# One transformer-like layer on Trainium2: the order of loads, place products and the first gate product between the output projection and the experts

## The chip, the cores and the metric

The kernel runs on one core of one Trainium2 chip, as one launch. The metric is the device time of one execution in microseconds (us), the median of several runs. Engines are named as in the profile: PE is TensorE, DVE is VectorE, ACT is ScalarE, POOL is GpSimd, SP is SyncE, which here only issues DMAs. A change of 1% of this kernel is about 10.5 us.

## What is computed

One layer of a hybrid encoder over 512 tokens (16 learned meta tokens are put ahead of the stream; 512 rows in the kernel, four blocks of 128) of width 1024, in float32. After two mixer branches (a chunked state-space scan and a causal pooling), gated and summed, the end of the layer is what matters here:

```python
    mixed = (gates[:, :, 0] * y_ssd + gates[:, :, 1] * y_pool) @ w_out[i]
    h = layer_norm(DN_ALPHA * h + mixed, ln1_g[i], ln1_b[i])
    ffn = moe_ffn(h, w_router, w_exp_gate[i], w_exp_up[i], w_exp_down[i])
    h = layer_norm(DN_ALPHA * h + ffn, ln2_g[i], ln2_b[i])
...
def moe_ffn(x, w_router, w_gate, w_up, w_down):
    scores = jax.nn.softmax((t @ w_router).astype(jnp.float32), axis=-1)
...
    topv, topi = lax.top_k(jnp.where(in_grp, scores, -1.0), TOP_K)
...
    for e in range(N_EXPERTS):
        h = jax.nn.silu(t @ w_gate[e]) * (t @ w_up[e])
        out = out + comb[:, e:e + 1] * (h @ w_down[e])
```

Each token is sent to 2 of 16 experts (hidden width 512), both within one of four groups of experts.

## The kernel before

**Stages.** The span of 1045 us has four parts: the input projection and the scan (to about 655 us), the output projection `wo` with residual, layer norm and router (656 to 733 us), the sixteen experts one after the other (735 to 1010 us), and the last layer norm.

**Output projection and router.** The product with `w_out` is cut into four blocks of tokens (`t`) and two halves of 512 columns (`hf`): `out_mm(t, hf)` is 24 matmuls of 128x512 into one PSUM bank, numbered 0 to 23, three for each of 8 blocks of the contraction (both operands are split into a high and a low part). All of `hf=0` comes first, then `hf=1`. `post(t, hf)` on DVE adds the bank to the residual `vt[t]` (in the trace `v`), which is loaded from `h_dram`, and gathers layer norm statistics. When both halves of a block are there, `router(t)` runs as a generator in stages: (0, 1) PE transposes `v`, ACT copies it to `hT`; (2) PE makes the logits (`ss<-wrg,hT`), DVE finishes the layer norm's scale, ACT takes the exponential (`e`), DVE picks the two experts (`oha`, `ohs`); then PE counts each token's place in its expert (`ss<-ohs,tri`, the rank product); (3) DVE makes from the ranks a one-hot matrix for the first expert's rows (`R0`, in the trace `xg`) and `R`; PE scatters tokens and weights into slots by `ss<-to,R` (the place product, a matrix `iw` of expert by slot). PE keeps program order here, and the table `AT[t]` says behind which matmul of `out_mm(t, 1)` which router takes its next stage: `(12,1)` is "ahead of matmul 12, a stage of router 1". So the blocks of matmuls are the cover under which the routers' DVE and ACT work runs.

**Start of the experts.** `place(t)` builds the first expert's tokens transposed by matmul (`pso<-xg,v`), and `x_out` writes them to `xT`, its first four blocks on ACT and the last four on DVE. The other experts' tokens are gathered by an indirect DMA on POOL from `h1_dram`, transposed on PE (`pt<-ident,xg`) and written by `x_out` as well. From `iw` DVE makes the lists of tokens `idx`, and PE's two small products `ss<-iws,xg` with two select masks spread the slots over partitions (`ixq`, `wq`); four products `ss<-ohs,onesb` count tokens for each expert. After that DVE multiplies the normed `vt` by `g1B`, adds `b1B`, POOL stores them in `o_dram`, where the experts' outputs are added later, and DVE works out a list of overflow (`ov`). For an expert `i`, PE makes a gate product (`gu`, into PSUM: 16 matmuls of 32x256 for each of the two halves of the weights; the trace records a float32 matmul twice), an up product, a third block of slots, transposes and the down product; ACT and DVE do the silu and the multiplication.

**Buffers and queues.** The masks live in `xg1` (its columns 512 to 767), a tile under the tag `hL2`, whose earlier user is `wo`; so their first write waits until PE has read that weight for the last time. POOL's queue holds, in program order, the masks' `iota`, then the loads of `v`, of the first up weights (`raw`), of `g1B` and `b1B`. Nearly all weights come over SP's queue, one 1 MB DMA a half, into a ring of buffers `places`; a DMA waits in SP's queue until the ring's next buffer is free, and everything behind it waits too. The scheduler sets the order on engines other than PE where no explicit order stands.

Of the kernel before, what the change touches and what calls it, by code (L numbers as in the profile page):

```python
# [10 lines left out]
F32 = mybir.dt.float32  # L11
# [4 lines left out]
AF = mybir.ActivationFunctionType  # L16
# [4 lines left out]
D = 1024  # L21
# [27 lines left out]
RX = 5  # L49
# [8 lines left out]
GX = 1  # L58
AT = ((), ((6,0),(8,0),(14,0)), ((6,1),(8,1),(12,0),(14,1),(20,0)), ((6,2),(8,2),(12,1),(14,2),(20,1)))
LASTS = (3,3,"0",3,"1",2,"2",2,3,"3",3)  # L60
# [32 lines left out]
def hybrid_kernel(ctx, tc, x, meta_tokens, ln_in_g, ln_in_b, w_router, w_in, conv_w, conv_b,  # L93
# [175 lines left out]
    with ExitStack() as p1:  # L269
# [613 lines left out]
        def mix(t):  # L883

            MARK(f"mix{t}")
            c = slice(t * 128, (t + 1) * 128)
            mt = ga.tile([128, 2, KT, 128], F32R, name="mt", tag=("ze", "XP", "yHL", "M")[t])
            mixT.append(mt)
            for i in range(2):
                k4 = slice(4 * i, 4 * i + 4)  # L890
                ps = mm()[:, 0, :].rearrange("p (k c) -> p k c", k=4) if (t, i) in MXP else ss((128, 4, 128))
                for k in range(4):
                    T.transpose(ps[:, k, :], acc[t][:, (4 * i + k) * 128:(4 * i + k + 1) * 128], ident)
                m = grp.tile([128, 4, 128], F32, name="mix", tag="y")
                for q in range(2):
                    V.tensor_mul(m[:, 2 * q:2 * q + 2], ps[:, 2 * q:2 * q + 2], sg0[2 * i + q][:, :, c])
                (G if (t, i) in MA else V).tensor_add(m, m, pooled[i][:, :, c])
                A.copy(mt[:, 0, k4], m)
                (G if (t, i) in MS else V).tensor_sub(mt[:, 1, k4], m, mt[:, 0, k4])
# [38 lines left out]
        xg1 = hpool.tile([128, D], F32, name="xg1", tag="hL2")  # L938
        for i, pat in enumerate(([[32, 2], [0, 2], [1, 32]], [[0, 4], [1, 32]])):
            sel = xg1[:, 512 + 128 * i:640 + 128 * i]  # L940
            G.iota(sel, pattern=pat, base=64 * i, channel_multiplier=0, **exact)
            V.tensor_scalar(sel, sel, tokf[:, 0:1], None, op0=OP.is_equal)
        hb = hpool.tile([128, 2, 2048], F32, name="hb", tag="hH")
        early = [hpool.tile([128, 4, 512], F32, name="rawh", tag="hL0"), hb[:, 0, :].rearrange("p (k c) -> p k c", k=4)]
        with tc.high_priority():
            G_ = InOrder(tc, G)
            for t in range(NT):
                (Q if t < QV else G_).dma_start(vt[t], h_dram[t * 128:(t + 1) * 128, :])
                if t == FX:
                    rows2(G_, first, wu[order[0]], 512)  # L950
                if t == GX:
                    G_.dma_start(g1B, bcast_row(ln1_g, D))
                    G_.dma_start(b1B, bcast_row(ln1_b, D))

# [123 lines left out]
        def place(t):  # L1078
# [5 lines left out]
            for k in range(KT):  # L1084
                T.matmul(xps[k // 4][:, k % 4, :CAP], lhsT=cols2(vt[t], k), rhs=R0s[t][:, :CAP],
                         start=(t == 0 and k % 4 == 0), stop=(t == NT - 1 and k % 4 == 3))

        exs, R0s, r0_ins, xps = [], [], [], []
        post(0, 0, pso0)
# [7 lines left out]
        for r in LASTS:  # L1097
            if isinstance(r, str):
                place(int(r))
            else:  # L1100
                next(stages[r])
        T = T_
        with tc.high_priority():
            x_out(xps, CAP)

        def to_idx(dst, src):
# [9 lines left out]
        for i in range(2):  # L1116
# [4 lines left out]
            V.tensor_copy(wq[i], pq[:, 2 * NE * i + NE:2 * NE * (i + 1)])  # L1121
        G.memset(xg1, 0.0)
        g1 = gather(xg1, h1_dram[:, :], idx[:CAP, order[1]:order[1] + 1]).ins
# [5 lines left out]
        V.tensor_copy(cnt, pn[:, :NE])  # L1129
        c1 = V.tensor_copy(ctab, cnt[0:1]).ins  # L1130

        with tc.issue_after(c1), tc.issue_after(g1):
# [16 lines left out]
    def tile_of(pool, tag, **kw):  # L1149
# [6 lines left out]
              + [hb_(1)] + [tile_of(ga, t) for t in ("ze", "XP", "yHL", "M")]  # L1156
              + [tile_of(wsp, t, **two) for t in ("wh", "wl")] * 2 + [tile_of(rawz, "raw")] * RZ
              + [tile_of(hpool, "hL0"), tile_of(wsp, "wh3", **one), hb_(0), tile_of(rawx[RX - 1], "raw")])

# [32 lines left out]

    def quad(p, lhs, rhs, m, **kw):

        for j in range(4):
            last_['PE'] = T.matmul(p[BK * j:BK * (j + 1), m], lhsT=lhs(j), rhs=rhs(j), **kw).ins


    gu3 = psG.tile([128, 256], F32, name="gu3", bufs=1)
    py3 = psY.tile([128, 256], F32, name="py3")  # L1200

    def gu(ws):

        MARK("gu")
        ps = psG.tile([128, 256], F32, name="gu")
        for n in range(KT):
            w, k = ws[n // 4], n % 4
            quad(ps, lambda j: xT[:, n, BK * (j // 2):BK * (j // 2) + BK],
                 lambda j: w[:, k, 256 * (j % 2):256 * (j % 2) + 256], slice(0, 256),
                 start=(n == 0), stop=(n == KT - 1))  # L1210
        return ps

# [314 lines left out]
    for i, e in enumerate(order[:last]):  # L1527
        if i:
            gather(XG[(i + 1) % 2], h1_dram[:, :], ix_of(i + 1))
        wg2, wu2 = (fetch(wg[e], 512), fetch(wu[e], 512)) if i else (wg_, wu_)  # L1530
        pg = gu(wg2)
        if i:
            count(i)
            htr(hs.pop(i - 1))
        pu = gu(wu2)
        hs[i] = act(pg, pu, p3=gu_third(i, (wg2, wu2)))
        xprep(XG[(i + 1) % 2])
        if i:
            add_rows(down(i - 1, fetch(wd[order[i - 1]], 256)), i - 1)
# [107 lines left out]
```

## Time and profile before

| quantity | value |
|---|---|
| runs | 1046.36, 1048.78, 1055.65 us; median 1048.78 |
| profiled execution | 1047.15 us |
| its span, first to last instruction | 1045.4 us |
| PE busy | 948.9 us, 91% of the span |
| DVE, ACT, POOL busy | 586.2, 350.5, 165.5 us |
| mean granted clock of TensorE | 0.966 |
| HBM read and written | 185.01 and 19.01 MB |

The span is 1.75 us shorter than the execution. In the profile a clock of 1.00 is 2.4 GHz, 0.50 is 1.2 GHz. A timeline row has the start, the duration of the whole row, engine, line of the kernel, operation, out and in, and in brackets the idle time of the engine before it with what released it; a row with x16 stands for sixteen instructions on end, the duration being that of all. A window row has its busy time for each engine with the count of instructions.

### The profile page before, as it was taken

Reading aid. Unit: us, or ns where it says so; the run is one execution under the profiler, and the core shown is the slowest. Engines: PE = TensorE matmul, PEld = TensorE weight load, DVE = VectorE, ACT = ScalarE, POOL = GpSimd, SP = SyncE. Lnnn points to the kernel's source line nnn. Section 1 sums busy time; section 2 is a strip of 40 time slices with the busy share of each in tenths; the row PEclk is TensorE's granted clock in tenths of the full one; section 3 lists DMA queues with packets and bytes.
Section 4 is the critical chain, followed back from the end, with each engine's and each line's share of the span. In section 5 each row is a group of like instructions: output and inputs, shape, how many; then the busy total and the mean of one; then the engine's idle time right before and its main releaser. Section 6 shows DMA issues by size and latency. Waiting matters only on the chain. (4 is left out here: it accounts for less than half of the span.)

```text
span 1045.4 us, 19947 instructions
## 1 busy us (share of the span) xinstructions
PE 948.9 (91%) x8460; PEld 762.1 (73%) x8460; DVE 586.2 (56%) x1159; ACT 350.5 (34%) x507; POOL 165.5 (16%) x147
## 2 busy tenths in 40 slices
PE   4879999999999999999999898979989788999970
PEld 3878888999899898989898776868655345664540
DVE  6877661476869697878788788456611101010143
ACT  4344333432534262524334353123212121212252
POOL 4830000000000000000000245100213121212223
PEclk9989999999999999999999998989999999999995
DMA  7442436422323241423332333787699999999854
GB/s 216 139 161 99 133 128 176 121 85 95 119 86 130 71 147 58 139 84 122 102 122 101 128 125 126 309 319 292 187 390 366 374 372 367 373 377 361 290 145 81
DMA packets 98291, 198.92 MB, mean 190 GB/s; under 512 B 9948, under 2 KB 56644, under 8 KB 97168
## 3 DMA queue, kind: packets, MB, share of 16 engines
q1 hardware_dynamic: 83248, 163.25, 44.5%
q0 software_dynamic: 9088, 18.63, 7.0%
q10 hardware_dynamic: 5856, 15.61, 4.0%
q8 instruction: 76, 1.25, 0.5%
q14 instruction: 23, 0.19, 0.1%
HBM read 185.01 MB, written 19.01 MB: 195 GB/s over the span
## 5 line engine op out<-in xcount | busy, mean ns | idle before, releaser
L255 DVE TENSOR_TENSOR wl<-raw,wh 128x2048 fp32r<-128x2048 f32 (+1 forms) x49 | 111.7, 2283 | 53.5 <-ACT wh L252 53.4
L89 PE MATMUL gu<-raw,xT 128*32 128x256 f32 (+1 forms) x2752 | 132.7, 343 | 6.2 <-issue 4.2
L252 ACT CAST wh<-raw 128x2048 fp32r<-128x2048 f32 (+1 forms) x49 | 87.9, 1798 | 144.9 <-PE ss L800 64.1
L307 PE MATMUL mm<-hH,wh 128*128 128x264 f32 x624 | 129.0, 288 | 6.0 <-ACT ze L599 5.3
L307 PE MATMUL mm<-hH,wl 128*128 128x264 f32 x624 | 128.3, 287 | 0.0
L307 PE MATMUL mm<-hL,wh 128*128 128x264 f32 x624 | 127.7, 286 | 0.0
L89 PEld LDWEIGHTS gu<-raw,xT 128*32 128x32 f32 x2752 | 87.7, 110 | 47.0 <-issue 13.8
L1254 DVE TENSOR_TENSOR sg<-sg,gu 128x128 f32<-128x128 f32 x15 | 4.3, 287 | 205.0 <-ACT sg L1253 205.0
L307 PEld LDWEIGHTS mm<-hH,wh 128*128 128x128 f32 x624 | 99.4, 190 | 9.3 <-ACT ze L599 5.5
L809 POOL TENSOR_TENSOR acc<-acc,pre 128x512 f32<-128x512 f32 x12 | 19.2, 1617 | 531.2 <-ACT pre L808 531.2
L325 PE MATMUL mm<-hH,wh 128*128 128x512 f32 x256 | 102.7, 401 | 0.0
L325 PE MATMUL mm<-hL,wh 128*128 128x512 f32 x256 | 101.7, 397 | 0.0
L325 PE MATMUL mm<-hH,wl 128*128 128x512 f32 x256 | 101.6, 397 | 0.0
L307 PEld LDWEIGHTS mm<-hH,wl 128*128 128x128 f32 x624 | 98.3, 190 | 1.2
L307 PEld LDWEIGHTS mm<-hL,wh 128*128 128x128 f32 x624 | 97.6, 190 | 0.2
L89 PE MATMUL py<-raw,hT 128*32 128x512 f32 (+1 forms) x672 | 70.4, 552 | 5.2 <-issue 5.2
L800 PE MATMUL ss<-wh,yy 128*128 128x512 f32 x192 | 67.4, 410 | 0.0
L1182 POOL DMA_INDIRECT o_dram<-ys,ixq x30 | 46.7, 1556 | 83.9 <-ACT ys L1337 74.5
L325 PEld LDWEIGHTS mm<-hH,wl 128*128 128x128 f32 x256 | 48.3, 188 | 10.4
L325 PEld LDWEIGHTS mm<-hH,wh 128*128 128x128 f32 x256 | 48.2, 188 | 10.2
L325 PEld LDWEIGHTS mm<-hL,wh 128*128 128x128 f32 x256 | 48.1, 188 | 10.3
L89 PEld LDWEIGHTS py<-raw,hT 128*32 128x32 f32 x672 | 22.2, 115 | 45.3 <-issue 39.9
(361 smaller groups left out, 1566.7 us busy)
## 6 DMA issues: line engine op xcount, KB each, us to landing
raw<-in_w_exp_down_dram SPq DMA_DIRECT2D x29, 1024.0 KB
raw<-in_w_in_dram SPq DMA_DIRECT2D x28, 1024.0 KB
raw<-in_w_exp_up_dram SPq DMA_DIRECT2D x28, 1024.0 KB
raw<-in_w_exp_gate_dram SPq DMA_DIRECT2D x27, 1024.0 KB
M<-aD ACTq DMA_DIRECT2D x8, 1024.0 KB
raw<-in_w_in_dram SPq DMA_DIRECT2D x16, 512.0 KB
raw<-in_w_ssd_out_dram SPq DMA_DIRECT2D x8, 1024.0 KB
ze<-eD ACTq DMA_DIRECT2D x16, 256.0 KB
```

What stands on the lines that cost most here:

```text
L89: return lambda *a, **k: self.tc.keep_in_program_order(f(*a, **k))
L252: A.copy(wh[:, c], src[:, c])
L255: (E[i] if E else V).tensor_sub(wl[:, c], src[:, c], wh[:, c])
L307: T.matmul(ps[:, i, :HF], lhsT=w[:, k, cs], rhs=h[k][:, i * HF:(i + 1) * HF], start=(n == 0), stop=(n == 3 * KT - 1))
L325: T.matmul(ps, lhsT=w[:, k, cs], rhs=h[k][:, NM:], start=(n == 0), stop=(n == 3 * KT - 1))
L800: T.matmul(ps, lhsT=y[:, j, t * 128:(t + 1) * 128], rhs=w[:, j, hf * 512:(hf + 1) * 512], start=(n == 0), stop=(n == 5))
L809: G.tensor_add(a, a, f)
L1182: return G.indirect_dma_start(out=dst, out_offset=off(ix), in_=src[:n], in_offset=None, **lim(dst), **kw)
L1254: V.tensor_mul(sg[:, 256:384], sg[:, 256:384], p3[:, 128:])
```

## The change

It has five parts:

- The loads of `v` are the first things in POOL's queue; the masks' `iota` and a memset of a quarter of `xg1` stand behind all loads, and the memset of the whole of `xg1` ahead of the first gather is gone.
- ACT runs an exponential on one column of `few` behind the last copy of `mt`, ahead of the routers.
- `AT`: router t-2's rank product stands behind 18 matmuls in place of 12 (and behind router t-1's logits), its place products behind 22 in place of 20, for t = 2 and 3 (the rows numbered from 0).
- The first half of expert 0's gate product (`pg0`) is written ahead of the products of `iws` and of the counts; it takes a bank of `psC` (`pso`). PE keeps program order to there.
- In the ring, `hL0`, `wh3`, `hb_(0)` and `rawx[4]` come ahead of the two `rawz`.

```diff
-AT = ((), ((6,0),(8,0),(14,0)), ((6,1),(8,1),(12,0),(14,1),(20,0)), ((6,2),(8,2),(12,1),(14,2),(20,1)))
+AT = ((), ((6,0),(8,0),(14,0)), ((6,1),(8,1),(14,1),(18,0),(22,0)), ((6,2),(8,2),(14,2),(18,1),(22,1)))
...
-                A.copy(mt[:, 0, k4], m)
+                last_[A] = A.copy(mt[:, 0, k4], m).ins
...
-        for i, pat in enumerate(([[32, 2], [0, 2], [1, 32]], [[0, 4], [1, 32]])):
-            sel = xg1[:, 512 + 128 * i:640 + 128 * i]
-            G.iota(sel, pattern=pat, base=64 * i, channel_multiplier=0, **exact)
-            V.tensor_scalar(sel, sel, tokf[:, 0:1], None, op0=OP.is_equal)
...
             for t in range(NT):
-                (Q if t < QV else G_).dma_start(vt[t], h_dram[t * 128:(t + 1) * 128, :])
-                if t == FX:
-                    rows2(G_, first, wu[order[0]], 512)
-                if t == GX:
-                    G_.dma_start(g1B, bcast_row(ln1_g, D))
-                    G_.dma_start(b1B, bcast_row(ln1_b, D))
+                G_.dma_start(vt[t], h_dram[t * 128:(t + 1) * 128, :])
+            rows2(G_, first, wu[order[0]], 512)
+            G_.dma_start(g1B, bcast_row(ln1_g, D))
+            last_[G] = G_.dma_start(b1B, bcast_row(ln1_b, D)).ins
+
+        with tc.issue_after(last_[G]):
+            G.memset(xg1[:, 768:], 0.0)
+            for i, pat in enumerate(([[32, 2], [0, 2], [1, 32]], [[0, 4], [1, 32]])):
+                sel = xg1[:, 512 + 128 * i:640 + 128 * i]
+                G.iota(sel, pattern=pat, base=64 * i, channel_multiplier=0, **exact)
+                V.tensor_scalar(sel, sel, tokf[:, 0:1], None, op0=OP.is_equal)
+
+        with tc.issue_after(last_[A]):
+            A.activation(few[:, 6:7], epsc, AF.Exp)
...
-        T = T_
         with tc.high_priority():
             x_out(xps, CAP)
+        pg0 = gu(wg_, psC.tile([128, 512], F32, name="pso")[:, :256])
...
-        G.memset(xg1, 0.0)
...
         c1 = V.tensor_copy(ctab, cnt[0:1]).ins
+        T = T_
...
-              + [tile_of(wsp, t, **two) for t in ("wh", "wl")] * 2 + [tile_of(rawz, "raw")] * RZ
-              + [tile_of(hpool, "hL0"), tile_of(wsp, "wh3", **one), hb_(0), tile_of(rawx[RX - 1], "raw")])
+              + [tile_of(wsp, t, **two) for t in ("wh", "wl")] * 2
+              + [tile_of(hpool, "hL0"), tile_of(wsp, "wh3", **one), hb_(0), tile_of(rawx[RX - 1], "raw")]
+              + [tile_of(rawz, "raw")] * RZ)
...
-        pg = gu(wg2)
+        pg = gu(wg2) if i else pg0
```

`gu` and `quad` are only moved up so that `pg0` can use them.

On POOL, between the last work on `mt` and the routers, the queue holds before (`v_5712` to `v_5715` are the four blocks of the residual, `xg` the tile with the masks):

```order
L899 TENSOR_TENSOR mt<-mix,mt 128x512 x2
L941 IOTA xg_5735 128x128 x2
L89 DMA v_5712<-h_dram 128x1024
L89 DMA v_5713<-h_dram 128x1024
L89 DMA raw<-in_w_exp_up_dram 128x2x1024
L89 DMA g1B<-in_ln_g_dram 128x1024
L89 DMA b1B<-in_ln_b_dram 128x1024
L89 DMA v_5714<-h_dram 128x1024
L89 DMA v_5715<-h_dram 128x1024
```

and with the change:

```order
L899 TENSOR_TENSOR mt<-mix,mt 128x512 x2
L89 DMA v_5712<-h_dram 128x1024
L89 DMA v_5713<-h_dram 128x1024
L89 DMA v_5714<-h_dram 128x1024
L89 DMA v_5715<-h_dram 128x1024
L89 DMA raw<-in_w_exp_up_dram 128x2x1024
L89 DMA g1B<-in_ln_g_dram 128x1024
L89 DMA b1B<-in_ln_b_dram 128x1024
L950 MEMSET xg_5735 128x256
L953 IOTA xg_5735 128x128 x2
```

The masks moved from ahead of seven loads to behind them, and the loads of `v` are now the first four.

On PE, within `out_mm(2, 1)`, from where router 0's rank product stands to its place products, before (`pso` is the output projection's bank, `tri` the triangle of ones):

```order
L89 MATMUL pso<-wh,mt 128x512
L89 LDWEIGHTS tri
L89 MATMUL ss<-ohs,tri 128x16
L89 MATMUL pso<-wh,mt 128x512
L89 MATMUL pso<-wl,mt 128x512
L89 MATMUL ss<-wrg,hT 128x16 x8
L89 MATMUL pso<-wh,mt 128x512 x2
L89 MATMUL pso<-wl,mt 128x512
L89 MATMUL pso<-wh,mt 128x512 x2
L89 MATMUL pso<-wl,mt 128x512
L89 MATMUL ss<-to_6058,R 128x32
L89 MATMUL ss<-to_6065,R 128x32
```

and with the change:

```order
L89 MATMUL ss<-wrg,hT 128x16 x8
L89 MATMUL pso<-wh,mt 128x512 x2
L89 MATMUL pso<-wl,mt 128x512
L89 MATMUL pso<-wh,mt 128x512
L89 LDWEIGHTS tri
L89 MATMUL ss<-ohs,tri 128x16
L89 MATMUL pso<-wh,mt 128x512
L89 MATMUL pso<-wl,mt 128x512
L89 MATMUL pso<-wh,mt 128x512 x2
L89 MATMUL ss<-to_6062,R 128x32
L89 MATMUL ss<-to_6069,R 128x32
```

The rank product now stands behind router 1's logits, with four matmuls between it and the place products; the same has moved in `out_mm(3, 1)` for routers 1 and 2.

On PE, at the start of the experts, before (`rawh` and `raww` are the two halves of expert 0's gate weights, `hb` and `raw` those of its up weights):

```order
L89 MATMUL ss<-to_6334,R 128x32
L1118 MATMUL ss<-iws,xg_5735 128x32
L1126 LDWEIGHTS onesb
L1126 MATMUL ss<-ohs,onesb 128x16
...
L1118 MATMUL ss<-iws,xg_5735 128x32
L89 MATMUL gu<-rawh,xT 32x256 x16
L89 MATMUL gu<-raww,xT 32x256 x16
L89 MATMUL gu<-hb,xT 32x256 x16
L89 MATMUL gu<-raw,xT 32x256 x16
```

and with the change:

```order
L89 MATMUL ss<-to_6336,R 128x32
L89 MATMUL pso<-rawh,xT 32x256 x16
L89 MATMUL pso<-raww,xT 32x256 x16
L89 MATMUL ss<-iws,xg_5735 128x32 x2
L89 LDWEIGHTS onesb
L89 MATMUL ss<-ohs,onesb 128x16
...
L89 MATMUL gu<-hb,xT 32x256 x16
L89 MATMUL gu<-raw,xT 32x256 x16
```

The gate product's 32 matmuls moved ahead of the products of the slots and counts.

## Rows read from the trace of the kernel before

**Rows 1.** Windows of two stretches: us; PE, PEld, DVE, ACT, POOL busy; PE clock, DMA share, GB/s.

```profile
682.00:712.00 30.00, 23.00 (x106) 19.31 (x106) 18.09 (x82) 8.34 (x17) 1.07 (x2) 0.83 0.67 261
...
860.00:1010.00 150.00, 140.19 (x2399) 83.38 (x2399) 20.75 (x55) 35.02 (x83) 37.60 (x28) 0.99 0.93 327
```

**Rows 2.** Timeline of PE: start, duration, operation, [idle before, releaser].

```profile
659.50 17.08 PE L89 MATMUL pso<-wo,mt 128*128 128x512 f32 x72
...
686.70 0.79 PE L89 MATMUL pso<-wh,mt 128*128 128x512 f32 x1 [4.50 <-DVE v L968]
...
702.90 0.18 PE L89 MATMUL ss<-ohs,tri 128*128 128x16 bf16 x1 [2.51 <-DVE ohs L1028]
...
703.49 3.29 PE L89 MATMUL ss<-wrg,hT 128*128 128x16 f32 x16
```

**Rows 3.** Windows of 2 us in the router's stretch, columns as in Rows 1.

```profile
672.00:674.00 2.00, 2.00 (x10) 1.63 (x9) 0.00 (x0) 0.00 (x0) 0.00 (x0) 1.00 0.04 8
686.00:688.00 2.00, 1.30 (x3) 1.11 (x4) 1.94 (x5) 0.00 (x0) 0.00 (x0) 0.64 1.03 414
688.00:690.00 2.00, 2.00 (x7) 1.51 (x7) 1.89 (x7) 0.00 (x0) 0.00 (x0) 0.51 1.02 406
704.00:706.00 2.00, 2.00 (x12) 2.00 (x11) 0.80 (x5) 0.00 (x0) 0.00 (x0) 0.50 0.00 0
...
710.00:712.00 2.00, 2.00 (x10) 1.69 (x10) 1.35 (x7) 0.90 (x4) 0.00 (x0) 0.89 0.65 262
```

**Rows 4.** Timeline of POOL, loads of the residual and of first weights.

```profile
676.49 0.47 POOL L941 IOTA xg<- 128x128 f32 x2 [19.82 <-PE pso L89]
...
678.37 0.73 POOL L89 DMA_DIRECT2D raw<-in_w_exp_up_dram  x1
```

**Rows 5.** Timeline of DVE, masks, residual sums and router 0.

```profile
676.79 0.49 DVE L942 TENSOR_SCALAR xg<-xg,tokf 128x128 f32<-128x128 f32 x2 [10.15 <-POOL xg L941]
685.36 0.69 DVE L968 SCALAR_TENSOR_TENSOR v<-v,ss 128x512 f32<-128x512 f32 x1 [8.08 <-DMA v<-h_dram]
...
702.62 0.23 DVE L1028 SCALAR_TENSOR_TENSOR ohs<-iota_r,fi,oha 128x16 bf16<-128x16 f32 x1
...
703.77 0.47 DVE L1064 TENSOR_SCALAR R<-iota_r,rank 128x128 f32<-128x128 f32 x2
```

**Rows 6.** Timeline of ACT, router 0's exponential.

```profile
695.11 1.28 ACT L998 ACT_TABLE_LOAD   x1 [3.28 <-DVE mn L995]
```

**Rows 7.** Timeline of PE, start of the experts.

```profile
732.86 0.56 PE L89 MATMUL ss<-to,R 128*128 128x32 f32 x4
...
735.69 1.93 PE L89 MATMUL gu<-rawh,xT 128*32 128x256 f32 x32
...
739.16 1.91 PE L89 MATMUL gu<-hb,xT 128*32 128x256 f32 x32
...
749.62 1.94 PE L89 MATMUL gu<-raw,xT 128*32 128x256 f32 x32 [0.16 <-issue]
...
760.65 1.88 PE L89 MATMUL gu<-raw,xT 128*32 128x128 f32 x48 [2.84 <-issue]
```

**Rows 8.** Timeline of DVE, start of the experts.

```profile
734.98 0.23 DVE L1119 TENSOR_SCALAR ixq<-ss,few 128x16 int32<-128x16 f32 x1 [0.42 <-PE ss L1118]
...
735.49 4.63 DVE L1134 TENSOR_TENSOR v<-v,g1B 128x1024 f32<-128x1024 f32 x4
...
749.19 1.23 DVE L1076 TENSOR_SCALAR xT<-pt,gb 128x96 f32<-128x96 f32 x4
```

**Rows 9.** Windows of 4 us in expert 1, columns as in Rows 1.

```profile
760.00:764.00 4.00, 3.35 (x60) 2.75 (x63) 0.62 (x2) 0.81 (x3) 0.00 (x0) 0.71 1.02 410
764.00:768.00 4.00, 4.00 (x37) 1.11 (x40) 1.23 (x4) 0.87 (x3) 0.96 (x1) 0.87 1.03 409
```

**Rows 10.** Timeline of SP's queue, the stop before expert 1's down weights.

```profile
721.01 0.51 SPq L228 DMA_DIRECT2D raw<-in_w_exp_up_dram  x1
746.62 4.78 SPq L1172 DMA_DIRECT2D raw<-in_w_exp_down_dram  x2
```

More of the change, by code (lines that the diff above doesn't have):

```diff
@@ L1086, in place, with quad, gu @@
                          start=(t == 0 and k % 4 == 0), stop=(t == NT - 1 and k % 4 == 3))
+        def quad(p, lhs, rhs, m, **kw):
+            for j in range(4):
+                last_['PE'] = T.matmul(p[BK * j:BK * (j + 1), m], lhsT=lhs(j), rhs=rhs(j), **kw).ins
+        def gu(ws, ps=None):
+            MARK("gu")
+            if ps is None:
+                ps = psG.tile([128, 256], F32, name="gu")
+            for n in range(KT):
+                w, k = ws[n // 4], n % 4
+                quad(ps, lambda j: xT[:, n, BK * (j // 2):BK * (j // 2) + BK],
+                     lambda j: w[:, k, 256 * (j % 2):256 * (j % 2) + 256], slice(0, 256),
+                     start=(n == 0), stop=(n == KT - 1))
+            return ps
         exs, R0s, r0_ins, xps = [], [], [], []
@@ L1191, in xprep @@
         x_out(ps, n)
-    def quad(p, lhs, rhs, m, **kw):
-        for j in range(4):
-            last_['PE'] = T.matmul(p[BK * j:BK * (j + 1), m], lhsT=lhs(j), rhs=rhs(j), **kw).ins
     gu3 = psG.tile([128, 256], F32, name="gu3", bufs=1)
     py3 = psY.tile([128, 256], F32, name="py3")
[L1202 to L1211, printed above, removed]
     def count(i):
```

## The prediction

> **What bounds the kernel now.** I read the page's busy shares, then windows, then the timelines of PE and of what releases it. PE is the bound: between 860 and 1010 us it is busy 140.19 of 150 us, between 682 and 712 us only 23.00 of 30, at a mean clock of 0.83 [rows 1]. So this stretch is where something is to be had, and the experts behind it follow PE's pace. The changed lines touch four gaps. PE stops at 682.20 (686.70 − 4.50) and waits 4.50 us for DVE's residual sum; later it waits 2.51 us for `ohs` [rows 2]. Behind both waits the granted clock falls to 0.50, which is 1.2 GHz against 2.4 at 1.00 [rows 3], so a wait is paid twice. At the experts' start PE goes from the last place product to the first gate product in 2.83 us (732.86 to 735.69), and in expert 1 it stops for 2.84 us with nothing that the profile shows as releaser [rows 7].
>
> **The change part by part.** All sums are against the profiled execution, 1047.15 us; the median of the runs is 1.6 us above it.
>
> *Loads of v.* DVE's first residual sum, at 685.36, had waited 8.08 us for the load of `v` [rows 5]. The load stood on POOL behind the masks' iota, which had waited 19.82 us, until 676.49, for PE's last read of the old tile [rows 4]. Now the seven loads are issued from 656.67 (676.49 − 19.82). At 0.73 us an issue, the longest kind there [rows 4], they take 5.1 us, to about 662, and at 672 to 674 the DMA engines are nearly idle, at 8 GB/s [rows 3], so `v` is there in time. Late next are the masks: iota at 676.5 behind a memset for which no row stands (two iotas of 128x128 take 0.47 us, I take as much at most), the masks until about 678. Then DVE's sum of block 0 is done by 679, but PE itself ends the product that the next sum needs at 682.20. That sum takes 0.69 us [rows 5], and 0.07 more pass as before: PE waits 0.76 us in place of 4.50. **−3.7** (0 if POOL doesn't run ahead, −4.5 at most). The short clock behind that wait goes too: (1−0.64)×1.30 + (1−0.51)×2.00 us of PE's busy time [rows 3] is **−1.45**.
>
> The Trainium skill, "SBUF — State Buffer", section "Who interferes with whom", says that GpSimd's DMA descriptors are starved while VectorE copies, casts or runs tensor_scalar in a two-port mode, not by tensor_tensor. By it the new place, 657 to 662 us, would be harmed if DVE ran copies there; the loads and the iota behind them would then come later: even at five times the issue time they end at 682, the masks 1 us and the sums 1.3 us behind that, so the term would be about −1.5 and the sum 1043. The rows of before show no issue in that stretch; those of 678 us, with DVE idle, can't decide it.
>
> *Table load.* 1.28 us of ACT [rows 6] leave router 0's chain from logits to `ohs`. ACT has room for them at 666, and the dummy exponential uses data at hand: nothing there.
>
> *Place products later.* Router 0's rank product waited 2.51 us [rows 2]. In the changed order six more matmuls and router 1's logits stand ahead of it. A matmul takes 0.237 us at full clock (17.08 us for 72), the logits half of 3.29 [rows 2], since they ran at 0.50 [rows 3]: 1.42 + 1.65 = 3.07 us of PE work, while `ohs`, which came at 702.85 [rows 5], comes 1.28 sooner against the logits. The slack is 3.07 + 1.28 − 2.51 = 1.8 us, so **−2.5**. The half clock behind it goes with it: three windows from 704 to 710 us with PE fully busy at 0.50 lose 3×1.0 us, the next 0.11×2.00 [rows 3], together **−3.2**.
>
> The cost is at the place products, 22 in place of 20 but now only four matmuls behind the rank product. DVE's chain from the rank product's end (702.90 + 0.18) to the end of `R` (703.77 + 0.47) [rows 2, 5] takes 1.16 us, and four matmuls cover 0.95. With DVE's other small operations in the way I take 0.5 us for each of two routers: **+1.0** (0 to 2.4, if R comes a whole chain late). Such a wait is far under the 2.51 us after which rows show the slow clock.
>
> *First gate product ahead.* The gate product can begin when place products and `xT` are done, at 732.86 + 0.56 = 733.4 in place of 735.69, 2.3 us earlier; its 3.47 us (735.69 to 739.16) [rows 7] then run ahead of the small products, which take about 0.7 (four in the trace as wide as the place products' four, 0.56, and four narrower ones), so the up product begins 1.6 us earlier. That gain isn't kept. On DVE `ixq`, at 734.98, opens a chain that runs without a gap (the multiplications by `g1B`, 4.63 us, as many additions, the overflow's small operations) up to the last four blocks of `xT` of expert 1 at 749.19 [rows 8]. `ixq` now waits for a product behind the gate: 733.4 + 3.47 + 0.4 (half of the small ones and DVE's pickup) = 737.3, so all of the chain is 2.4 us later. PE's second half of expert 1's gate product, at 749.62 [rows 7], needs that `xT`: it starts at 752.0, **+2.4**, and PE, done with the first half 1.6 us earlier (at 747.9), stands still for some 4.1 us before it. After such waits the clock halves; the nearest price is that behind the 2.84 us stop: 0.29×3.35 + 0.13×4.00 [rows 9], **+1.5** (0 to 3.2).
>
> *The stop without a releaser.* The 2.84 us at 760.65 [rows 7] have their operands at hand. If they belong to PE's instruction stream, the new wait just ahead gives it time to catch up, and they shrink with their slow clock (1.5); if not, they stay. I take half of the 2.84: **−1.4** (0 to −4.3).
>
> *Ring and queue.* SP stops after 721.5 until 746.62 [rows 10], because the ring's next buffers, `rawz`, wait for the stores of `v`. Now four buffers that PE alone frees come first, so weights flow again some 10 us earlier, and the two `rawz` stand later. Expert 1's first weights were there before, and the experts follow PE, so **0** on the path, up to −3 if some part of PE's remaining idle time is a weight.
>
> The sum: −3.7 − 1.45 − 2.5 − 3.2 + 1.0 = −9.9 up to the experts, +2.4 + 1.5 − 1.4 = +2.5 there: −7.4. That is 1039.8 on the profiled execution and 1041.4 on the median; I say **1041**.
>
> **The rivals.** *The gains arrive whole.* If the stop of 2.84 us is absorbed with its slow clock and the wait on DVE stays (+2.4 + 1.5 − 4.3), the experts' start costs nothing, and the change gives 10.3 us: 1038. If besides the earlier weights give 3 us: 1035. For it: the stop names no releaser. Against: the new wait comes at another instruction, 10 us earlier.
>
> Beside this stands the Trainium skill, "Runtime: NRT & Kernel Launch", section "Instruction fetch mechanics": instructions are fetched in blocks, in sequence, and a taken branch outside the window stalls the engine. By it the stop is one of fetching, and the wait ahead would hide it; the trace names no cause.
>
> *The wait only moves (slower).* The rank product's new cover feeds nothing if DVE is late with `R`, which now stands behind the next router's operations on DVE, among them two that wait for ACT's exponential. If the place products wait 2.5 us, the shortest wait after which rows show the slow clock [rows 2, 3], each of the two places costs 2.5 + 3.2 us: 11.4 in place of 1.0. With the experts' wait (+3.9, nothing absorbed) the sum is −10.9 + 11.4 + 3.9 = +4.4: 1053. It decides when the chain of 1.16 us grows past 3.4. Against it: the operations added are like `ohs`, 0.23 us each [rows 5].
>
> *The change doesn't do what it says.* If `v` still comes late (its loads find no free issue, or the masks hold DVE), 5.1 us are missing: −2.3, 1046.
>
> **How the numbers follow.** The forecast, 1041 with its own spread of 1039 to 1045: 0.55. Gains whole: 0.25 at 1038, and 0.05 at 1035. Late `v`: 0.08. The moved wait: 0.07. The bounds of the terms reach from about −14 to −2. The range **1034 to 1047** leaves out the moved wait and a few deeper gains. A measurement of this kernel can tell about 1%, 10.5 us, from no change: faster means under 1038.3. Of the whole gains something over half lies there, and the weights' case, and a tail of the forecast: 0.30. Slower than 1059 asks for more than the moved wait's price: 0.03, with a little added for what no row shows: **0.05**. Within 1%: **0.65**.
>
> **What would show it.** Right: PE's wait of 4.50 us under 1, no wait at the rank product, clock 1.00 from 686 to 712 us of before's stretch, two waits under 1 us at `ss<-to,R`, POOL's loads by 662; and a new wait of about 4 us in expert 1's gate product with the clock down behind it. Wrong: `v` late still; a wait over 2 us at `ss<-to,R`; no wait in expert 1, if the scheduler's DVE order lets `xT` pass; a different length of the experts' stretch, which I hold unchanged.

## The result and the profile after

The changed kernel takes 1040.8 us (median of 20 runs, 1036.98 to 1046.41) against 1048.08 us of the kernel before (20 runs, 1042.04 to 1055.65): a ratio of 0.9926, 95% interval 0.9906 to 0.9947, 7.3 us by the medians. The forecast was 1041, the range 1034 to 1047.

Single executions of one kernel differ by 10 us and more, so two profiles can't be laid on each other by the clock of their spans. In the profile after, the first output product (`pso<-wo,mt`, 72 in a row) starts at 657.01 us, in that of before at 659.50 [rows 2], though of all that was changed only the first two loads of `v` stand ahead of it; over the twelve further profiles that start lies anywhere between 656.06 and 662.66. So every comparison below counts from that start.

| us after the start of the first output product | before | after | gain |
|---|---|---|---|
| last place product ends | 73.92 | 63.41 | 10.5 |
| first gate product starts | 76.19 | 63.33 | 12.9 |
| expert 0's up product starts | 79.66 | 68.16 | 11.5 |
| second half of expert 1's gate product starts | 90.12 | 82.70 | 7.4 |
| expert 2's transposes (`pt<-ident,xg`) start | 102.95 | 93.74 | 9.2 |
| the last expert's down product (`pye`) starts | 349.92 | 345.54 | 4.4 |
| end of the span | 385.90 | 380.09 | 5.8 |

PE's timeline after, at the places of [rows 2], shows the wait for the residual sum at 0.78 us in place of 4.50, and none at the rank product and the place products:

```profile
679.32 0.39 PE L89 MATMUL pso<-wh,mt 128*128 128x512 f32 x1
680.49 0.50 PE L89 MATMUL pso<-wh,mt 128*128 128x512 f32 x1 [0.78 <-DVE v L972]
...
695.73 0.18 PE L89 MATMUL ss<-ohs,tri 128*128 128x16 bf16 x1
...
697.01 0.60 PE L89 MATMUL ss<-to,R 128*128 128x32 f32 x4
```

The windows after (columns as in [rows 1]) answer to its first row with a PE busy for 29.59 of 30 us at a clock of 1.00, where before it was 23.00 at 0.83; in the experts PE is no busier than before:

```profile
682.00:712.00 30.00, 29.59 (x189) 25.08 (x187) 23.26 (x129) 11.46 (x26) 1.63 (x3) 1.00 0.79 290
...
860.00:1010.00 150.00, 138.98 (x2215) 80.69 (x2207) 23.30 (x61) 36.81 (x85) 36.58 (x27) 0.97 0.87 305
```

POOL's timeline after, answering to [rows 4]: the loads of `v` are out by 662.04 and the masks stand where they stood, behind PE's last read. Two loads waited for DVE, whose `mix` had to leave the memory first, and that cost nothing:

```profile
654.10 1.34 POOL L89 DMA_DIRECT2D v<-h_dram  x2
659.32 0.54 POOL L89 DMA_DIRECT2D v<-h_dram  x1 [3.88 <-DVE mix L896]
661.51 0.53 POOL L89 DMA_DIRECT2D v<-h_dram  x1 [1.65 <-DVE mix L896]
...
673.92 0.31 POOL L950 MEMSET xg<- 128x256 f32 x1 [10.10 <-PE pso L89]
674.19 0.47 POOL L953 IOTA xg<- 128x128 f32 x2
```

PE's timeline after at the experts' start, answering to [rows 7]. The first gate product follows the place products without a gap; the wait forecast for expert 1's gate product is there with 4.21 us, the product behind it takes 3.23 us in place of 1.94 at the fallen clock, and the 192 matmul records from 743.35 run through without the stop that stood at 760.65 before:

```profile
719.86 0.56 PE L89 MATMUL ss<-to,R 128*128 128x32 f32 x4
720.34 1.93 PE L89 MATMUL pso<-rawh,xT 128*32 128x256 f32 x32
...
725.17 1.93 PE L89 MATMUL gu<-hb,xT 128*32 128x256 f32 x32
...
739.71 3.23 PE L89 MATMUL gu<-raw,xT 128*32 128x256 f32 x32 [4.21 <-DVE sg L1257]
...
743.35 7.15 PE L89 MATMUL gu<-raw,xT 128*32 128x256 f32 x192
750.75 1.17 PE L89 MATMUL pt<-ident,xg 96*128 96x96 f32 x8 [0.25 <-DMA xg<-h_dram,idx]
```

DVE's timeline after, answering to [rows 8]: the chain from `ixq` to `xT` is later. Counted from the end of the last place product, the first `ixq` comes 2.4 us later than before (at 3.96 us, before at 1.56), and `xT` 3.1 us later (18.86 against 15.77): the second pair of `ixq` and `wq`, which stood behind the multiplications before (at 740.03), now stands ahead of them, and DVE waits for it.

```profile
724.38 0.23 DVE L1140 TENSOR_SCALAR ixq<-ss,few 128x16 int32<-128x16 f32 x1 [2.83 <-PE ss L89]
...
725.20 0.23 DVE L1140 TENSOR_SCALAR ixq<-ss,few 128x16 int32<-128x16 f32 x1 [0.50 <-PE ss L89]
...
739.28 1.23 DVE L1080 TENSOR_SCALAR xT<-pt,gb 128x96 f32<-128x96 f32 x4
```

So up to expert 2 the gain is 9.2 us in the two profiles; then 4.8 of it are lost between expert 2's transposes and the last down product, which take 247.0 us before and 251.8 after. The experiments were to say which part brought what, and what takes it back in the experts.

### The profile page after: what moved, and what is told of

Read it like the earlier page. It is cut to its first block, busy times and chain, and to the rows that moved or that the text cites. A ratio compares the mean times of both kernels' runs of the same rounds, so it can differ in the third digit from the quotient of the medians.

```text
span 1037.1 us, 19952 instructions
## 1 busy us (share of the span) xinstructions
PE 947.8 (91%) x8460; PEld 756.9 (73%) x8460; DVE 584.2 (56%) x1159; ACT 350.4 (34%) x508; POOL 165.6 (16%) x147
## 5 line engine op out<-in xcount | busy, mean ns | idle before, releaser
L89 PEld LDWEIGHTS gu<-raw,xT 128*32 128x32 f32 x2656 | 85.1, 110 | 54.2 <-issue 18.2
L89 PE MATMUL py<-raw,hT 128*32 128x512 f32 (+1 forms) x704 | 74.1, 559 | 5.4 <-issue 4.7
L325 PEld LDWEIGHTS mm<-hH,wl 128*128 128x128 f32 x256 | 48.2, 188 | 10.5
```

The costliest lines, as they stand in the source:

```text
L89: return lambda *a, **k: self.tc.keep_in_program_order(f(*a, **k))
L325: T.matmul(ps, lhsT=w[:, k, cs], rhs=h[k][:, NM:], start=(n == 0), stop=(n == 3 * KT - 1))
```

## The experiments

All twelve kernels start from the changed kernel, but for before_light, which starts from the kernel before. Places are again counted from the start of the first output product.

### The parts undone one at a time

The control, the changed kernel again.

> The changed kernel as it is, on the same chip as the three others of this group. Both theories: ratio to the kernel before 0.990 to 0.995 (some 1041 us). From the first output product to the end of the last place product, 63.4 us (73.9 before); PE waits about 4.2 us in expert 1's gate product.

Measured: 1040.63 us (12 runs), ratio 0.9922 (0.9894 to 0.9950); 63.40 us to the end of the last place product, the wait on DVE 4.22 us, expert 2's transposes at 93.54, 251.96 us from there to the last down product. Its stretches repeat those of the first profile to 0.2 us, though it starts 5.4 us later.

**Loads of v (no_loads).**

```diff
-        with tc.issue_after(last_[G]):
-            G.memset(xg1[:, 768:], 0.0)
...
+        G.memset(xg1[:, 768:], 0.0)
+        for i, pat in enumerate(([[32, 2], [0, 2], [1, 32]], [[0, 4], [1, 32]])):
...
+                if t == 1:
+                    rows2(G_, first, wu[order[0]], 512)
+                    G_.dma_start(g1B, bcast_row(ln1_g, D))
+                    G_.dma_start(b1B, bcast_row(ln1_b, D))
```

> The changed kernel, with the masks ahead of the loads of v on POOL and the loads in the old order. My account: PE waits 4.5 us again for the residual sum in place of 0.8 and runs at half clock behind it, so from the first output product to the last place product it takes 68.6 us in place of 63.4, and about 1046 us in all (ratio 0.9975). Rival (the transfers are hidden anyway, because later work waits for something else): the 3.7 us come back at the place products, 63.4 to 65 us, 1041 to 1042 us.

Measured: 1045.21 us, ratio 0.9985 (0.9960 to 1.0010), and 68.74 us to the last place product, 5.3 more than the control. PE's timeline of this run, at the residual sum and behind it:

```profile
684.47 0.63 PE L89 MATMUL pso<-wh,mt 128*128 128x512 f32 x1 [4.46 <-DVE v L971]
...
701.28 0.18 PE L89 MATMUL ss<-ohs,tri 128*128 128x16 bf16 x1
```

The wait and (by its windows, 0.55 and 0.60 for 4 us) the slow clock are back; the rank product doesn't wait. The part is worth what the prediction gave it: 5.3 of the 10.5 us won ahead of the experts, and 4.6 us of the end time by the medians.

**Table of place products (no_at), and with it the early table load (no_at_table).**

```diff
-AT = ((), ((6,0),(8,0),(14,0)), ((6,1),(8,1),(14,1),(18,0),(22,0)), ((6,2),(8,2),(14,2),(18,1),(22,1)))
+AT = ((), ((6,0),(8,0),(14,0)), ((6,1),(8,1),(12,0),(14,1),(20,0)), ((6,2),(8,2),(12,1),(14,2),(20,1)))
... (no_at_table alone:)
-        with tc.issue_after(last_[A]):
-            A.activation(few[:, 6:7], epsc, AF.Exp)
```

> The changed kernel with the old table of place products; the exponential's table is still loaded ahead. My account: router 0's rank product waits again at matmul 12 of block 2, but only 2.5 - 1.3 = 1.2 us, since 1.28 us have left its chain, and a wait of this length leaves the clock at 1.00: +1.2 us, less 0.3 for the short waits at the place products that go, 64.3 us to the last place product and about 1042 us. Rival: the wait comes back whole with its slow clock, as if the table load had been hidden anyway: +5.5 us, 69 us and about 1046 us.

> The changed kernel with the old table of place products and without the exponential's table loaded ahead; the loads of v stay early. My account: router 0's rank product waits 2.5 us again and half clock follows: +5.5 us, about 69 us from the first output product to the last place product, 1046 us. Rival (the wait was a result of the late residual and went with it): 63.4 to 65 us, 1041 to 1042 us.

Measured: no_at 1037.99 us, ratio 0.9904 (0.9871 to 0.9936), 63.20 us to the last place product; no_at_table 1039.96 us, ratio 0.9919 (0.9888 to 0.9950), 64.10 us. The rank product's row in no_at:

```profile
693.47 0.18 PE L89 MATMUL ss<-ohs,tri 128*128 128x16 bf16 x1 [0.17 <-DVE ohs L1032]
```

and in no_at_table, with the window behind it:

```profile
692.84 0.18 PE L89 MATMUL ss<-ohs,tri 128*128 128x16 bf16 x1 [1.09 <-DVE ohs L1030]
```

```profile
694.00:696.00 2.00, 2.00 (x16) 1.86 (x16) 0.80 (x4) 0.00 (x0) 0.00 (x0) 1.00 0.01 2
```

Both of my expectations were too dear, the second by 5 us. With `v` there in time, the old table waits 1.09 us, not 2.51, at full clock, and the early table load alone takes away nearly all of that. So 1.4 of the 2.51 us, and the slow clock behind it, had come from the late residual itself. DVE's timeline of the kernel before shows how: sums and statistics of other blocks, late as block 0's, stand in router 0's chain between `e` and `ohs`, 3.2 us in these rows (in no_at_table one sum and one statistic of 0.68 us each stand there):

```profile
697.68 1.28 DVE L968 SCALAR_TENSOR_TENSOR v<-v,pso 128x512 f32<-128x512 f32 x2
...
699.02 1.28 DVE L969 BATCH_NORM_STATS2 sta<-v 128x6 f32<-128x512 f32 x2
700.22 0.67 DVE L968 SCALAR_TENSOR_TENSOR v<-v,pso 128x512 f32<-128x512 f32 x1
```

no_loads shows the other side: with the new table and the early table load, the rank product doesn't wait even where `v` is late. Two remedies for one wait: undone one at a time, neither is missed.

**First gate product ahead (no_pg0).**

```diff
+        T = T_
         with tc.high_priority():
             x_out(xps, CAP)
-        pg0 = gu(wg_, psC.tile([128, 512], F32, name="pso")[:, :256])
...
-        T = T_
...
-        pg = gu(wg2) if i else pg0
+        pg = gu(wg2)
```

> The changed kernel with the first gate product behind the products of the slots and counts, as before. My account (the stop of 2.84 us without a releaser is a load of instructions that the wait on DVE hid): the gate product starts 2.3 us later, the wait of 4.2 us in expert 1's gate product and its slow clock (1.3) go, but the stop without a releaser comes back near the end of expert 1's up product, some 2.8 us with a slow clock of 1.4: within 2 us of the changed kernel, 1040 to 1042 us. Rival (the stop had another cause, which the change removed): no stop, 1036 to 1038 us.

Measured: 1036.79 us (6 runs), ratio 0.9896 (0.9849 to 0.9943), the time that the rival gave; the interval overlaps the control's, so that this part alone costs time is not shown. The gate product starts 2.7 us later, the wait on DVE is gone, and of the stop without a releaser 0.94 us is there, not 2.8: expert 2's transposes come at 92.83 in place of 93.5 to 93.7. That is 0.8 of the 3.8 us between the medians; the rest lies in later experts, which take 248.1 us in this profile. This run also pays for something that the kernel before doesn't show: the gate product ran at half clock from its start, behind a wait of 1.12 us (the second row's 32 matmuls take 3.64 us where [rows 7] has 1.93):

```profile
721.55 0.57 PE L1139 MATMUL ss<-iws,xg 128*128 128x32 f32 x2 [1.12 <-DVE iws L1133]
...
723.09 3.64 PE L89 MATMUL gu<-rawh,xT 128*32 128x256 f32 x32
```

**The ring (no_ring).** The two `rawz` stand again ahead of the four buffers that PE frees.

```diff
-              + [tile_of(hpool, "hL0"), tile_of(wsp, "wh3", **one), hb_(0), tile_of(rawx[RX - 1], "raw")]
-              + [tile_of(rawz, "raw")] * RZ)
+              + [tile_of(rawz, "raw")] * RZ
+              + [tile_of(hpool, "hL0"), tile_of(wsp, "wh3", **one), hb_(0), tile_of(rawx[RX - 1], "raw")])
```

> The changed kernel with the ring in its old order, the two buffers that wait for the stores of v first. My account: SP starts again some 3 to 5 us later, when the first stores of v have landed, expert 1's weights are there all the same, and the time is that of the changed kernel within 2 us, 1039 to 1043 us. Rival (the weights set the experts' pace): each us that SP starts later is a us of the end, 1044 to 1046 us.

Measured: 1042.03 us, ratio 0.9929 (0.9901 to 0.9958), expert 2's transposes at 94.75, 1.2 us later than in the control, which is in the noise of the end time. Whether it is worth 1 us or nothing can't be told. Nor does the run bring SP's stop back: SP's queue starts again 72.7 us after the first output product, as in the profile after (72.8) and not as before (87.1), with the weights for the buffers that PE frees ahead of the others here too; its waits for the stores of `v` are 14.9 us in both, 28.9 before. Rows of no_ring, then of the profile after:

```profile
731.52 1.24 SPq L228 DMA_DIRECT2D raw<-in_w_exp_gate_dram  x2
...
744.15 8.14 SPq L1194 DMA_DIRECT2D raw<-in_w_exp_down_dram  x4
```

```profile
729.77 1.24 SPq L1194 DMA_DIRECT2D raw<-in_w_exp_down_dram  x2
```

So whether the weights would set the pace with a later start, as the rival has it, this run doesn't test. In the profiles of the kernels with all weights, no wait of PE over 1 us in the experts up to the last down product is put down to a weight's DMA.

### What takes the wait's place

**Overflow behind xT (ov_late).** DVE's small operations for the overflow, which stood ahead of expert 1's `xT`, go behind it.

```diff
     adds = []
-    overflow()
...
         xprep(XG[(i + 1) % 2])
+        if not i:
+            with tc.issue_after(last_[V]):
+                overflow()
```

> The changed kernel with the overflow's small operations moved on DVE from ahead of expert 0's multiplication and expert 1's xT to behind them. My account: xT no longer stands behind 3.8 us of them; of the wait of 4.2 us in expert 1's gate product about 0.5 stays and the slow clock behind it goes, -5 us there; but a load of PE's instructions lies in this very place, so a stop without a releaser of up to 3 us shows in its stead or in expert 1's up product: -1 to -5 us, 1036 to 1040 us. Rival (what is gained ahead of the experts is given back there, because the weights set the pace): 1040 to 1042 us, the gain gone by expert 8.

Measured: 1039.82 us, ratio 0.9916 (0.9889 to 0.9944); expert 2's transposes at 93.47, as in the control. PE's timeline of this run shows why:

```profile
735.25 1.93 PE L89 MATMUL gu<-raw,xT 128*32 128x256 f32 x32 [0.26 <-DVE xT L1080]
...
749.99 1.52 PE L89 MATMUL pt<-ident,xg 96*128 96x96 f32 x8 [4.50 <-DMA xg<-h_dram,idx]
```

The wait on DVE fell from 4.2 to 0.26 us, and 4.50 us of waiting for the gather of expert 2's tokens came in its place: POOL had issued it at 736.43, behind the stores of `v`, and PE could go on with it 13.6 us later, with the DMA engines full (share 1.04 from 737 to 750 us). The 0.25 us at the same place in the profile after was its tip. My expectation had looked for a stop for instructions there, of which 0.39 us is left (at 743.91), and missed the gather.

**The gather ahead of the stores (gather_early),** on top of ov_late. Its buffer must not share memory with `v`, so it takes one that had held `mt`, and the ring has one place less.

```diff
         g1 = gather(xg1, h1_dram[:, :], idx[:CAP, order[1]:order[1] + 1]).ins
+        xg0 = ga.tile([128, 2, D], F32, name="xg0", tag="M")[:, 0, :]
+        with tc.issue_after(g1):
+            G.memset(xg0, 0.0)
+        g1 = gather(xg0, h1_dram[:, :], idx[:CAP, order[2]:order[2] + 1]).ins
...
-        if i:
+        if i > 1:
             gather(XG[(i + 1) % 2], h1_dram[:, :], ix_of(i + 1))
...
-              + [hb_(1)] + [tile_of(ga, t) for t in ("ze", "XP", "yHL", "M")]
+              + [hb_(1)] + [tile_of(ga, t) for t in ("ze", "XP", "yHL")]
```

> The run ov_late with expert 2's tokens gathered into a buffer of the ring (one of those that held mt, now no longer in the ring) ahead of the stores of v on POOL, in place of behind them. My account (in ov_late the gather, which landed 12.5 us after its issue, took the place of the wait on DVE): expert 2's transposes no longer wait 4.5 us for it and come 88.5 to 90 us after the first output product in place of 93.5, and the end is 4 to 5 us sooner than ov_late's: 1034 to 1037 us. Rival (stops in later experts take it back, or the ring's missing buffer slows the weights): 1038 to 1041 us.

Measured: 1034.49 us (6 runs, 1030.94 to 1038.58), ratio 0.9868 (0.9837 to 0.9900); expert 2's transposes at 88.26. Its PE runs through:

```profile
733.67 3.70 PE L89 MATMUL gu<-raw,xT 128*32 128x256 f32 x64
737.30 0.55 PE L89 MATMUL pt<-ident,sg 128*128 128x128 f32 x3
737.78 7.26 PE L89 MATMUL gu<-raw,xT 128*32 128x256 f32 x192
744.98 1.20 PE L89 MATMUL pt<-ident,xg 96*128 96x96 f32 x8
```

This is the fastest version found, 6 us under the changed kernel. With DVE's chain and the gather both out of the way, expert 2 is reached 5.3 us sooner than in the control. There is no stop for instructions in expert 1 either, at a clock of 1.00.

**Two parts left out (no_pg0_at),** the edits of no_pg0 and no_at together.

> The changed kernel without two of its parts, the first gate product ahead and the new table of place products; the early loads of v, the table load ahead and the ring stay. My account: 63.2 us to the last place product, expert 2's transposes at 92.6 us, no wait on DVE: 1035 to 1038 us, as good as or better than the changed kernel by 3 to 5 us. Rival (the medians of no_at and no_pg0 below the changed kernel's were chance): 1040 to 1042 us.

Measured: 1036.38 us (6 runs), ratio 0.9885 (0.9858 to 0.9912); 63.20 us to the last place product, expert 2's transposes at 90.64. So early loads, early table load and ring alone give by the medians more than the whole change. Here the gate product ran at full clock, behind a wait of 1.11 us:

```profile
724.25 1.93 PE L89 MATMUL gu<-rawh,xT 128*32 128x256 f32 x32
```

### What is lost in the experts

**Half the weights (light, before_light, light_no_pg0).** These kernels leave out half of the weights of experts 1 to 14, so they compute something else; PE's instructions stay. The edit in all three, without its lines in the third block and the down product; light_no_pg0 has that of no_pg0 besides.

```diff
-                rows2(Q, r, src, u * n)
+                rows2(Q, r[:, :2 * q], src, u * n)
...
-                w, k = ws[n // 4], n % 4
+                w, k = ws[n // 4], n % 2
...
-        wg2, wu2 = (fetch(wg[e], 512), fetch(wu[e], 512)) if i else (wg_, wu_)
+        wg2, wu2 = (fetch(wg[e], 512, 1), fetch(wu[e], 512, 1)) if i else (wg_, wu_)
```

> The changed kernel with only half of the weights of experts 1 to 14 loaded, each loaded half being used twice, so that PE's instructions are the same and the DMA engines half empty; it leaves out half of those weights and computes something else. Both: the stops of PE without a releaser of 1.4 to 4 us in the experts shrink. My account (instruction loads stand behind weights on the DMA engines): the instruction loads go on at the same rate, none is followed by a stop over 0.5 us, the clock stays at 1.00 and the experts take 12 to 20 us less than the changed kernel's 282. Rival (the stops are loads of instructions that come late by their own latency or by branches, whatever the traffic): stops of 2 to 4 us stay, less than 5 us are won.

> The kernel before with half of the weights of experts 1 to 14 left out, as in the run light (it computes something else). My account (in the experts nothing is given back but stops for instruction loads behind crowded DMA engines): without such stops, the experts from expert 2's transposes to the last product take as long as in the run light, 226.5 us within 1; expert 2's transposes come 100 us after the first output product (92.6 there), so the whole difference of some 7.5 us is left at the end: 1022 to 1024 us against 1015.8. Rival (part of what is gained ahead is lost to something else in the experts, as 4.8 us were in the profiles of the full kernels): 1018 to 1021 us.

> The run light with the first gate product behind the products of the slots and counts, as before; half of the weights of experts 1 to 14 left out too. My account now (the first gate product ahead costs more than it gives, by the wait on DVE in expert 1): expert 2's transposes come about 91 us after the first output product in place of 92.6, and 1.5 to 2 us less in all, 1014 us. Rival (the part costs nothing, the 3.9 us won in the run no_pg0 came from stops that fell otherwise): 1015.5 to 1018 us.

Measured: light 1015.75 us, before_light 1024.23, light_no_pg0 1013.65 (4, 5 and 4 runs). Windows of the changed kernel, then of light (columns as in [rows 1]):

```profile
760.00:860.00 100.00, 86.65 (x1273) 47.84 (x1266) 11.11 (x36) 19.89 (x52) 21.83 (x17) 0.92 1.04 374
860.00:960.00 100.00, 95.52 (x1610) 56.15 (x1606) 9.26 (x30) 19.27 (x49) 24.43 (x18) 0.97 1.03 369
```

```profile
760.00:860.00 100.00, 96.24 (x1496) 54.73 (x1488) 12.97 (x42) 23.42 (x61) 26.85 (x20) 1.00 0.81 245
860.00:960.00 100.00, 96.68 (x1700) 59.06 (x1696) 11.13 (x36) 20.98 (x54) 25.64 (x19) 1.00 0.70 212
```

With DMA share 0.7 to 0.8 in place of 1.03, the same PE instructions run at a clock of 1.00 with PE busy 96 to 97 of 100 us; from expert 2 to the last down product they take 226.5 us, not 251.8. The stops over 1 us that are put down to nothing or to PE's own sequencer, seven in the profile after (1.38 to 4.19 us), are down to one of 1.89 us, and that one stands near expert 12 in every run (1.5 to 2.1 us). So the others come from the traffic. Three of the seven (4.19, 1.46 and 1.72 us) and the one left are put down to PE's sequencer at L1234, the conditional branch past the third block of slots, where an expert skips that block; at four other experts the same branch costs 0.18 us. Rows of the profile after, then of light:

```profile
783.26 1.17 PE L89 MATMUL pt<-ident,xg 96*128 96x96 f32 x8 [0.18 <-PEq L1234]
802.13 1.52 PE L89 MATMUL pt<-ident,xg 96*128 96x96 f32 x8 [4.19 <-PEq L1234]
```

```profile
922.22 1.17 PE L89 MATMUL pt<-ident,xg 96*128 96x96 f32 x8 [1.89 <-PEq L1234]
```

That the stops are loads of instructions is an inference from three things. Before's stop at 760.65 [rows 7] lies in the third block of slots, which reads weights that the same expert's earlier products had just read, so no weight can have been late. And each of the stops over 1.4 us up to 880 us, five in the profile before and five in that after, has a load of instructions in it or begun at most 2 us ahead of it; the DMA view of the kernel before, 756 to 758 us, for that stop (packets, MB, share of 16 engines; `q8` is the queue of instructions):

```profile
q1 hardware_dynamic: 105, 0.43, 90.4%
...
q8 instruction: 1, 0.02, 3.5%
```

With a load every 6 us or so, such a meeting alone would often be chance; the end of the stops says more. By the packets of that queue in the traces, all seven stops of the profile after end 2.3 to 2.7 us after a load of 16 KB began (at 802.13 a load from 799.62, at 942.23 one from 939.5), and the one left in light 2.7 us after. A load takes about 1.0 us in light as in the profile after, so it isn't its own transfer that grows long; what makes it come late under full traffic no run shows.

There are as many such loads in the experts of light, 39 from 736 to 978 us:

```profile
q8 instruction: 39, 0.64, 1.1%
```

and 37 from 733 to 978 us of the profile after. The Trainium skill, "Runtime: NRT & Kernel Launch", section "Instruction fetch mechanics", says that instructions are loaded in sequence in blocks of 16 KiB, and that this is mostly hidden. The size agrees (0.64 MB in 39 loads); that it is hidden holds here, but for the stop near expert 12, where the DMA engines have room, and not where weights fill them.

The light kernels show the change without most stops: 8.5 us by the medians. Expert 2's transposes come 8.6 us apart (101.25 and 92.63), of which some 1.5 us is before_light's first gate product at a clock of about 0.5 (8.40 us from its start to the third block, 6.93 in the kernel before); the experts take 227.6 and 226.5 us: nothing is given back, a little is won. In these profiles the first gate product ahead costs: without it expert 2's transposes come at 90.08 in place of 92.63, the last down product 1.3 us sooner; the 2.1 us between the medians rest on four runs each and are not clear of noise.

## Why the prediction was right, and where it wasn't

The time was right, and the terms ahead of the experts in their sum, 10.5 us against 9.9. Within both sums errors of opposite sign met. Term by term:

- **Loads of v, −3.7 and −1.45.** Right: the wait is 0.78 us (0.76 forecast), the clock 1.00; no_loads puts the pair at 5.3 us. Starved descriptors did no harm here: two issues took 1.34 us beside DVE's tensor_tensor work at 654 us, and 1.33 us before, at 677 us, with DVE idle from 677.28 on. By the rule on them ("SBUF — State Buffer", "Who interferes with whom", in the Trainium skill) tensor_tensor doesn't starve them, and the trace agrees; copies at that place are shown by no run.
- **Place products later, −2.5 and −3.2.** The times vanished, but the step gave them to the wrong part. It took the rank product's wait of 2.51 us as one of its own, to be covered by 3.07 us of matmuls and 1.28 us of table load. no_at_table measured that 1.4 us of it, and all of its slow clock, go with the late residual, so table and table load add 0.7 us to the early loads (64.10 against 63.40), not 5.7. The terms of two remedies were added as if they met two waits.
- **New waits at the place products, +1.0.** Mis-sized: under 0.1 us; `R` was ready within the four matmuls' cover. The rival in which this wait moves didn't come.
- **First gate product ahead, +2.4 and +1.5.** The mechanism is right: a wait of 4.21 us (4.1 forecast) for the chain of DVE's operations, 1.3 us of slow clock, a gain of 7.4 us at that point (7.5). That the gain agrees to 0.1 us is luck: the term of +2.4 (by its own figures 2.3) measured 3.1 us, since 10.5 us were won ahead and 7.4 are left. The first `ixq` is later by 2.4 us as forecast; the 0.7 more is the second pair, which DVE now takes ahead of the multiplications. The up product gained 1.0 us by itself, not 1.6. What the step missed is that the gather for expert 2 limits the next place to about the same time; ov_late shows it. So the wait's removal bought nothing by itself.
- **The stop without a releaser, −1.4.** Mis-sized: it went whole with its slow clock, so expert 2 came 9.2 us earlier and not 7.4. The reason given, that the new wait lets PE's instructions catch up, is borne out only in part: without that wait PE stops at the same matmul for 0.94 us in no_pg0, 1.14 in no_pg0_at and 0.39 in ov_late, but not at all in gather_early, and nowhere for 2.84.
- **Ring and queue, 0.** SP starts again at 72.8 us in place of 87.1, 14 us earlier where some 10 were forecast. no_ring, in which it starts at 72.7, doesn't undo that, so what it is worth no run shows.
- **Experts unchanged, 0.** Wrong in the profiles: 247.0 us before, 251.8 and 252.0 after. Between expert 2 and the last down product the kernels that load all weights spread from 246.97 to 252.31 us, in no order of what they had gained ahead: 248.7 for no_loads, 247.0 for no_at, 248.1 for no_pg0, 248.7 for gather_early, 252.3 for no_ring; two profiles of the changed kernel agree to 0.2 us. By the medians the change gives 7.3 us, by the two profiles 5.8, so on the average of runs less may be lost than these two show. Light shows that most of what lies above 226 us is stops under full traffic and their slow clock. Why they fall so that the changed kernel pays 4.8 us more than before stays open: it would need each stop's place against each transfer. So two of the misses (the stop, the experts) had opposite signs, and the forecast's closeness owes something to that.

## What to carry to other kernels

A wait behind a late load can be the child of that load, as here: a step that covers the second wait and a step that removes the first can't both be paid in full, and only undoing the pair shows it. Before a product is moved ahead of small ones, follow what those small ones open on another engine, and behind that the next late thing (here a gather behind stores). Here moving the product, or the product and DVE's small operations, bought nothing that can be told from noise; with the gather moved too, 6 us came. What the product adds there by itself no run shows. Where single executions spread by 1%, count from an event that the change doesn't touch, and take away the disturbing traffic in a side kernel to see the rest.

## What the hardware showed that was not expected

- With full DMA engines PE stops in the experts for 1.4 to 4.2 us at a time, seven times in the profile after, and behind five of these stops the clock is 0.50 within 4 us; all but one of them fall under 1 us when the engines have room: with 212 to 245 GB/s in place of 370 the same instructions took 25 us less.
- A gather of 96 rows, issued at 736.43 in ov_late, let PE go on 13.6 us later (749.99) while the engines were full.
- All seven stops end 2.3 to 2.7 us after a load of 16 KB of instructions began, under full traffic and, for the one left, with room.
- Much the same gap gave either clock: the place ahead of the first gate product, with a wait of 1.11 to 1.12 us, was followed by 0.50 in no_pg0, by 1.00 in no_pg0_at and before. What tells the two apart no run here shows.
